# Row norms taken block by block, a third bank for separate products, gate weights split in every chunk, and both z products beside attention, in a two-layer trunk kernel

## The chip, the cores and the metric

The kernel runs on one core of one Trainium2 chip. The metric is the device time of one execution in microseconds. Before the change the median of three runs is 2850.37 us, the lowest 2839.6 and the highest 2852.43.

## The reference

A sequence of 2048 tokens with 1024 channels goes through two layers. Everything is float32. Layer 0 mixes by trailing means, layer 1 by a strictly causal "stick-breaking" attention with 16 heads of 64 channels. Both layers end with a gated embedding.

```python
# layer 0
h = rms_norm(x, a_norm);  u, z = split(h @ a_w_in)
pooled = trailing_means(u, windows 2, 4, 8, 16) - u        # one window per group of 256 channels
x = x + (einsum(pooled, a_w_group) * a_scale * silu(z)) @ a_w_out
x = x + (p[0] @ ple_w[0]) * sigmoid(x @ ple_gate_w[0])
# layer 1
k, v = split(rms_norm(x, kv_norm) @ w_kv);  k = rms_norm_per_head(k, k_norm)
q, z = split(rms_norm(x, b_norm) @ b_w_in); q = rms_norm_per_head(q, b_q_norm)
logits = q k^T / 8          # for s < t only
A[t,s] = sigmoid(logits[t,s]) * prod over s<j<t of (1 - sigmoid(logits[t,j]))
x = x + ((A @ v) * silu(z)) @ b_w_out
x = x + (p[1] @ ple_w[1]) * sigmoid(x @ ple_gate_w[1])
```

## The kernel before, in words

**Tiles.** Activations lie transposed: 128 channels on the partitions, 512 tokens along the free axis. The sequence is cut into four chunks of 512 tokens, numbered 0 to 3. To keep float32 accuracy in matmuls that take a shortened format, every operand is split into a high half (a cast on ScalarE) and a low half (source minus high half, on POOL or VectorE; `split`, lines 187 to 194, and `put_split` for weights, lines 206 to 216). Each product of two tiles is three matmuls: high by high, high by low, low by high. A weight unit of two 128-row tiles is a pair of halves in the pool `wpair`; `pump` (line 250) keeps up to nine units in flight along a list, `plan`. A raw weight goes through a ring of four buffers, `io`, that it shares with residual tiles and others. A unit that is marked `keep` is stored split to memory (`once`) after its first use, and later loads read 512 KB of halves from there; a unit that is not kept is read raw (256 KB) and split again.

**Order of the work.** `opening` does layer 0 for the chunks 0 and 1, then `pair_part(0, 1)`: the v, k and q of both chunks. `attend` then sweeps the heads of the chunks 0 to 2 and threads a stream of other products between the steps of attention: z of chunk 1, and layer 0 of the chunks 2 and 3 except for the gate of chunk 3 (`beside_first`). `middle` does that gate and `pair_part(2, 3)`. The second `attend` does the heads of chunk 3, with z of chunk 3 and the layer ends of the chunks 0 to 2 beside it. The layer end of chunk 3 is last.

**The pair's products.** `job` (line 922) computes v, then k, then q for two chunks at once by a scheme of seven products of half the size instead of eight: p1 to p7, each 48 matmuls of 512 columns. Their operands are mixtures of the activations, which `build` (line 850) makes on VectorE and splits, and mixtures of the weights, which were made once and stored (`mixed`). Some products are added in place in four banks (`total`); p2, p3 and p5 are needed apart and go to the two banks `psl` (`own`). `evacuate` (line 895) reads them out. Ahead of the job `pair_part` computes z of the first chunk of the pair (`gate_z`, line 799), 192 matmuls, while `build` makes its sums.

**The row norms.** `keyed` (line 734) gets four blocks of 128 tokens one after another. For each it squares (ScalarE) and sums by head (VectorE, 8 columns). After the fourth block `rsqrt_mean` (line 177) takes the root of all 32 columns on POOL, as a power of minus one half, and VectorE multiplies the four blocks. The transposes (`finish`) are queued by a list, `lag`, at the earliest 44 steps of TensorE later. They use the two banks `psa`.

**Values.** Attention needs differences of successive rows of v. `valued` (line 709) stores a block of v to memory, loads it back one row later, and POOL subtracts (line 726).

**Order on the engines.** Within one engine instructions run in the order in which they stand. The framework's scheduler sets that order, except that TensorE's instructions in a job and in attention, and the weights' casts, keep the order of the program.

## Time and profile before

| What | Value |
|---|---|
| Profiled execution, its own time | 2840.63 us |
| Its span, first to last instruction | 2838.6 us |
| Mean granted TensorE clock | 0.981 |
| Median of the runs | 2850.37 us |
| Instructions | 38319 |
| Bytes moved | 652.77 MB |

Names in the rows: PE is TensorE, DVE is VectorE, ACT is ScalarE, POOL is GpSimd, SP is SyncE, which issues nearly all transfers. In a group, "out<-in" are the tiles written and read, then come the shapes and the count; behind the first bar are the busy time of all and the mean of one in ns; behind the second is the idle time of the engine ahead of these instructions, and what ended it. In a timeline row the first number is the start and the second the time until the last of the merged instructions ended; matmuls overlap, so the pace is read from start to start. In a row of waits stand the waiting engine, tile and line, what it waited for, the sum, the count and the longest.

`psd`, `psl`, `pso`, `psa` are banks; `total` and `own` are the tiles of the seven products, `pst` is a bank of transposes or of a norm's small sums, `xs` and `xw` are split and raw operands of the job, `rq` is the reciprocal norm of a row, `qs` a block of v, k or q.

### The profile page before, as it was taken

The page shows a single profiled execution, that of the slowest core. Times are in us where ns is not written, and L with a number is a line of the kernel's source. Part 1 is how long each engine was busy: PE and PEld are TensorE (multiplying, and loading weights), DVE is VectorE, ACT ScalarE, POOL GpSimd, SP SyncE. Part 2 cuts the span into 40 slices and gives each one's busy share as a digit, 9 for nine tenths or more (in the row PEclk, how much of TensorE's full clock was granted, in tenths as well). Part 3 has the DMA queues.
Part 4 walks back from the last instruction along what each step waited for, and adds up shares of the span by engine and source line. Part 5 has one row for each costly group of instructions (what it writes and reads, how often), then busy time and mean ns, then how long its engine had stood idle before and what let it go on. Part 6 is the DMA issues. An engine that isn't in the chain of part 4 may idle for free.

```text
span 2838.6 us, 38319 instructions
## 1 busy us (share of the span) xinstructions
PE 2696.2 (95%) x13118; PEld 2215.0 (78%) x13118; DVE 1946.6 (69%) x2479; ACT 1431.3 (50%) x2838; POOL 1038.0 (37%) x737
## 2 busy tenths in 40 slices
PE   9988999889899999999998989999999999999999
PEld 7866888777678887778886777788878878888887
DVE  6733726435458877788545354689999989999952
ACT  5444214345566656545424454566656555666531
POOL 1458513566664425332436655401120111112111
PEclk9999999999999999999999999999999999999999
DMA  7899678575688878767685846865645564566454
GB/s 258 307 401 381 227 243 312 167 248 160 189 308 301 276 246 275 267 214 248 240 284 158 267 148 180 295 188 189 236 157 189 179 208 147 181 192 219 164 186 163
DMA packets 315935, 652.77 MB, mean 230 GB/s; under 512 B 47710, under 2 KB 80478, under 8 KB 315740
## 3 DMA queue, kind: packets, MB, share of 16 engines
q1 hardware_dynamic: 315164, 649.53, 67.6%
q8 instruction: 104, 1.70, 0.2%
q10 hardware_dynamic: 576, 0.79, 0.1%
q14 instruction: 91, 0.75, 0.1%
HBM read 474.56 MB, written 175.64 MB: 229 GB/s over the span
## 4 chain that ended last, share of the span: by engine, by line
PE 37%; DVE 8%; POOL 3%; issue 3%; DMA 3%; ACT 2%; SPq 0%; POOLq 0%; DVEq 0%; ACTq 0%
PE psd L51 18%; PE pso L51 6%; PE psa L55 6%; PE psl L51 6%; DVE pp L1102 4%; DVE at L1122 2%; POOL rq L181 1%; DMA vraw<-qs 1%; POOL xs L189 1%; PE own L51 1%; POOL wpair L210 1%; DVE qs L748 1%; DMA vs<-vraw 0%; ACT at L1120 0%; DVE sg L704 0%
## 5 line engine op out<-in xcount | busy, mean ns | idle before, releaser
L1102 DVE TENSOR_TENSOR_SCAN pp<-pp,floor 128x512 f32<-128x512 f32 (+3 forms) x640 | 752.1, 1211 | 9.5 <-ACT pp L1098 9.5
L1120 ACT CAST at<-psa 128x512 fp32r<-128x512 f32 (+3 forms) x640 | 303.0, 525 | 374.0 <-PE psa L55 371.3
L51 PE MATMUL psd<-x,wpair 128*128 128x512 f32 x1728 | 441.5, 399 | 18.7 <-ACT sg L700 7.7
L1122 DVE TENSOR_TENSOR at<-psa,at 128x512 fp32r<-128x512 f32 (+3 forms) x640 | 358.8, 598 | 138.2 <-ACT at L1120 136.5
L51 PEld LDWEIGHTS psd<-x,wpair 128*128 128x128 f32 x1728 | 328.5, 192 | 96.4 <-ACT sg L700 9.2
L51 PE MATMUL pso<-at,vv 128*128 128x512 f32 (+3 forms) x1280 | 329.2, 371 | 36.6 <-DVE at L1122 32.5
L1098 ACT ACTIVATE pp<-psl 128x512 f32<-128x512 f32 (+3 forms) x640 | 312.9, 550 | 10.3 <-PE psl L51 9.5
L51 PEld LDWEIGHTS pso<-at,vv 128*128 128x128 f32 x1280 | 228.8, 188 | 111.9 <-DVE at L1122 63.7
L51 PE MATMUL psd<-xp,wpair 128*128 128x512 f32 x1248 | 304.3, 392 | 0.4 <-DVE wpair L215 0.2
L55 PE MATMUL psa<-ident,pp 128*128 128x128 f32 x2176 | 294.1, 275 | 0.0
L51 PE MATMUL total<-wpair,xs 128*128 128x512 f32 x1152 | 286.5, 405 | 5.5 <-DVE zr L804 4.2
L55 PEld LDWEIGHTS psa<-ident,pp 128*128 128x128 f32 x2176 | 254.5, 141 | 27.0
L51 PEld LDWEIGHTS psd<-xp,wpair 128*128 128x128 f32 x1248 | 231.8, 188 | 51.0 <-DVE wpair L215 1.4
L1145 POOL TENSOR_TENSOR os<-os,zt 128x512 f32<-128x512 f32 x32 | 54.2, 1694 | 587.6 <-ACT os L1144 540.4
L51 PEld LDWEIGHTS total<-wpair,xs 128*128 128x128 f32 x1152 | 222.1, 196 | 53.5 <-DVE zr L804 5.0
L51 PE MATMUL psl<-kk,qa 128*128 128x512 f32 (+3 forms) x640 | 259.2, 410 | 0.0
L51 PE MATMUL psl<-kk,qb 128*128 128x512 f32 (+3 forms) x640 | 235.2, 368 | 0.0
L51 PE MATMUL own<-wpair,xs 128*128 128x512 f32 x864 | 215.1, 405 | 17.6 <-ACT qs L901 11.2
L51 PEld LDWEIGHTS own<-wpair,xs 128*128 128x128 f32 x864 | 166.7, 196 | 57.4 <-ACT qs L901 15.0
L51 PE MATMUL psd<-og,wpair 128*128 128x512 f32 x744 | 187.7, 392 | 0.0
L51 PE MATMUL psd<-mp,wpair 128*128 128x512 f32 x768 | 181.7, 393 | 3.8 <-ACT wpair L208 3.3
L51 PEld LDWEIGHTS psd<-mp,wpair 128*128 128x128 f32 x768 | 144.7, 189 | 35.3 <-ACT wpair L208 3.7
(145 smaller groups left out, 3998.3 us busy)
## 6 DMA issues: line engine op xcount, KB each, us to landing
wpair<-once SPq DMA_DIRECT2D x348, 512.0 KB, 4.8
kk<-kd SPq DMA_DIRECT2D x160, 256.0 KB, 3.2
vv<-vd SPq DMA_DIRECT2D x160, 256.0 KB, 3.3
once<-wpair SPq DMA_DIRECT2D x68, 512.0 KB, 6.3
wpair<-wf SPq DMA_DIRECT2D x48, 512.0 KB, 5.6
once<-kp SPq DMA_DIRECT2D x36, 512.0 KB, 4.7
vd<-vv SPq DMA_DIRECT2D x32, 512.0 KB, 5.4
kd<-hl SPq DMA_DIRECT2D x64, 256.0 KB, 3.7
```

Source lines behind the costliest of these rows:

```text
L51: return held_in_order(nc.tensor.matmul(*a, **k))
L55: return held_in_order(nc.tensor.transpose(*a, **k))
L181: G.tensor_tensor(out=out_ap, in0=ms, in1=neghalf[:, 0:w], op=ALU.pow)
L189: low = lambda: lo.tensor_tensor(out=half_of(pr, 1), in0=src, in1=f(half_of(pr, 0)), op=ALU.subtract)
L210: (G if state["lo"] % 3 and not state["boot"] else V).tensor_tensor(out=pr[:, 1], in0=raw, in1=f(pr[:, 0]), op=ALU.subtract)
L748: V.tensor_tensor(out=q8, in0=q8, in1=rq[:, 8 * i : 8 * i + 8].unsqueeze(2).to_broadcast([P, 8, HD]), op=ALU.mult)
L1098: A.activation(out=pp[:, r0:], in_=ps[:, :w], func=AF.Sigmoid, scale=-1.0)
L1102: V.tensor_tensor_scan(out=pp[:, r0:][:, ::-1], data0=pp[:, r0:][:, ::-1], data1=least, initial=1.0 if st["diag"] else st["carry"][j], op0 ...
L1120: A.copy(out=at[:, 0, cs], in_=pt[:, cs])
L1122: return lambda: V.tensor_tensor(out=at[:, 1, cs], in0=pt[:, cs], in1=f(at[:, 0, cs]), op=ALU.subtract)
L1145: G.tensor_tensor(out=os, in0=os, in1=zt, op=ALU.mult)
```

## The change

There are five edits.

1. `keyed` takes the root of each block's 8 columns and multiplies that block at once. Four roots of 8 columns stand in place of one of 32.
2. The products apart take turns over three banks: two of `psl` and one of `psa`, from the pair that the transposes use. For v the order of the products is p1, p2, p5, p6, p3, p7, p4.
3. The gate and embedding weights of layer 0 (20 units a chunk) are not kept: no store after the first chunk, and a raw load and a split in every chunk.
4. z of the first chunk of a pair is no longer computed ahead of the job but in the attention after it, ahead of z of the second chunk. `build` takes four of its steps ahead of the job and the others, the splits for p4, in it. It uses the raw tiles that `prefill` left (two loads a step instead of four, into the pool `tmp`). p5's low halves are now split on VectorE. The job's tail reloads all eight tiles of the first chunk, and the attention stream reloads the eight of the second.
5. `prep`, which loads the next chunk's input, puts its norm on the list `lag` when it runs beside attention.

```diff
     def plan_a(s):
-            plan_block("ag", gate_a, b, keep=True)
-            plan_block("al", ple_a, b, keep=True, order=PAIRS[:1])
+            plan_block("ag", gate_a, b)
+            plan_block("al", ple_a, b, order=PAIRS[:1])
...
+    FIRST_PRODUCTS = ("p1", "p2", "p5", "p6", "p3", "p7", "p4")
...
     def keyed(s, kind, b, j, qs):
+        q8 = qs.rearrange("q (h d) -> q h d", d=HD)
         A.activation(out=sq, in_=qs, func=AF.Square)
-        V.tensor_reduce(out=ss[:, 8 * j : 8 * j + 8], in_=sq.rearrange("q (h d) -> q h d", d=HD), op=ALU.add, axis=AX.X)
+        V.tensor_reduce(out=ss, in_=sq.rearrange("q (h d) -> q h d", d=HD), op=ALU.add, axis=AX.X)
+        rsqrt_mean(rq, ss, HD, "q")
+        V.tensor_tensor(out=q8, in0=q8, in1=rq.unsqueeze(2).to_broadcast([P, 8, HD]), op=ALU.mult)
         if j < 3:
             return
-        rsqrt_mean(rq, ss, HD, "q")
-        for i, qs in enumerate(rows):
-            q8 = qs.rearrange("q (h d) -> q h d", d=HD)
-            V.tensor_tensor(out=q8, in0=q8, in1=rq[:, 8 * i : 8 * i + 8].unsqueeze(2).to_broadcast([P, 8, HD]),
-                            op=ALU.mult)
...
     def job(c0, c1):
-                    ps = bank("psl", "own") if apart else totals[j]
+                    if apart:
+                        owns[0] += 1
+                    ps = bank(("psl", "psl", "psa")[owns[0] % 3], "own") if apart else totals[j]
...
     def build(s):
         raws = sets.pop("raw")
         for i in range(4):
-            loads = [scaled(c, kt, row) for c, kt in ((c0, i), (c1, i), (c1, 4 + i), (c0, 4 + i))]
+            (a21, scale1), (a22, scale2) = scaled(s, i, tmp), scaled(s, 4 + i, tmp)
+            a11, a12 = raws[i], raws[4 + i]
...
-            split(sets["p5"][i], a22, G)
+            split(sets["p5"][i], a22, V)
...
     def pair_part(c0, c1):
-        side = build(c0, c1)
-        yield from every(gate_z(c0, sets["p1"] + sets["p2"]), 40, side)
         state["hold"] = True
-        side = reload(c1, 4)
+        side = build(c1)
+        for _ in range(4):
+            next(side)
+        back = reload(c0)
         for n, _ in enumerate(job(c0, c1)):
...
     def beside_first():
-        yield from every(gate_z(1, chunk[1]["x2"]), 18, chunk[2].setdefault("side", prep(2)))
+        yield from z_part(0, reload(1))
+        yield from z_part(1, prep(2))
```

The orders below show three places of the first pair. The first is TensorE, where the job begins. In these rows `psd<-xs` is z of chunk 0, `pst<-ones,acc` and `pst<-ident,r` are the norm of chunk 1, `total` and `own` are p1 and p2. Before:

```order
L51 MATMUL psd<-ple,wpair 128x512 x6
L51 MATMUL psd<-xs,wpair 128x512 x37
L51 MATMUL pst<-ones,acc 128x1 x4
L51 MATMUL psd<-xs,wpair 128x512 x26
L55 MATMUL pst<-ident,r 128x128 x4
L51 MATMUL psd<-xs,wpair 128x512 x129
L51 MATMUL total<-wpair,xs 128x512 x48
```

Now, on the same engine:

```order
L51 MATMUL psd<-ple,wpair 128x512 x6
L51 MATMUL pst<-ones,acc 128x1 x4
L55 MATMUL pst<-ident,r 128x128 x4
L51 MATMUL total<-wpair,xs 128x512 x48
L51 MATMUL own<-wpair,xs 128x512 x96
L51 MATMUL total<-wpair,xs 128x512 x48
```

The 192 matmuls of z have gone, and the norm's matmuls follow the gate's directly; `own` x96 is p2 and p5.

The second place is POOL in the first products of the job. `xs_...` are low halves of the sums, the line with `vs` is the subtraction of shifted values of p2's blocks, and `wpair` is a weight's low half; wpair_4365 is p5's second weight. Before, POOL had this order there:

```order
L189 TENSOR_TENSOR xs_4302<-xw_4632,xs_4302 128x512
L189 TENSOR_TENSOR xs_4301<-xw_4638,xs_4301 128x512
L210 TENSOR_TENSOR wpair_4693<-wraw_4694,wpair_4693 128x512
L210 TENSOR_TENSOR wpair_4771<-wraw_4772,wpair_4771 128x512
L210 TENSOR_TENSOR wpair_4779<-wraw_4780,wpair_4779 128x512
L726 TENSOR_TENSOR vs_4810<-vs_4810,qs_4807 128x512
```

Now POOL has this order:

```order
L189 TENSOR_TENSOR xs_4282<-xw_4277,xs_4282 128x512
L189 TENSOR_TENSOR xs_4307<-xw_3918,xs_4307 128x512
L735 TENSOR_TENSOR vs_4410<-vs_4410,qs_4407 128x512
L189 TENSOR_TENSOR xs_4306<-xw_4131,xs_4306 128x512
L735 TENSOR_TENSOR vs_4428<-vs_4428,qs_4425 128x512
L189 TENSOR_TENSOR xs_4305<-xw_4300,xs_4305 128x512
L210 TENSOR_TENSOR wpair_4365<-wraw_4366,wpair_4365 128x512
```

The weights' low halves stood ahead of the first value subtraction; now p5's second one stands behind two of them.

The third place is VectorE in k, around the first group of norms. L740 and L749 are the sums by head, L748 and L751 the multiplies by `rq`, the L215 and L210 rows are weights. Before:

```order
L740 TENSOR_REDUCE ssq<-sqq 128x8
L215 SCALAR_TENSOR_TENSOR wpair<-wraw,gains,wpair 128x512 x2
L740 TENSOR_REDUCE ssq<-sqq 128x8
L748 TENSOR_TENSOR qs<-qs,rq 128x512 x4
L210 TENSOR_TENSOR wpair<-wraw,wpair 128x512
```

Now, on VectorE:

```order
L749 TENSOR_REDUCE ssq<-sqq 128x8
L911 TENSOR_TENSOR qs<-total,qs 128x512
L215 SCALAR_TENSOR_TENSOR wpair<-wraw,gains,wpair 128x512
L749 TENSOR_REDUCE ssq<-sqq 128x8
L751 TENSOR_TENSOR qs<-qs,rq 128x512
L215 SCALAR_TENSOR_TENSOR wpair<-wraw,gains,wpair 128x512
L210 TENSOR_TENSOR wpair<-wraw,wpair 128x512
L751 TENSOR_TENSOR qs<-qs,rq 128x512 x2
```

The multiplies stood together behind the last sum; now two of four stand behind it, and two weights' low halves stand between.

More of the change, by code (lines that the diff above doesn't have):

```diff
@@ L280, in plan_kinds @@
             b0 = 2 if kind == "v" else 0
-            for name in PRODUCTS:
+            for name in FIRST_PRODUCTS if kind == KINDS[0] else PRODUCTS:
                 for i in range(4):
@@ L533, in prep, with total, spread @@
             yield
-        r = token_norm(ck["acc1"], "x")
-        yield
-        ck["rb1"] = bcast(r, "x")
-        yield
+        if state["solo"]:
+            ck["rb1"] = bcast(token_norm(ck["acc1"], "x"), "x")
+            return
+        def total():
+            ck["r1"] = token_norm(ck["acc1"], "x")
+        def spread():
+            ck["rb1"] = bcast(ck["r1"], "x")
+        lag.append((time["now"] + 12, total))
+        lag.append((time["now"] + 24, spread))
     def gated_late(zr, sg):
@@ L870, in build @@
             split(sets["p3"][i], a12, G)
+            split(sets["p7"][i], a21, G)
+            yield
+        for i in range(4):
+            raw, scale = scaled(s, 4 + i, tmp)
+            yield
+            scale()
+            sets["p4"].append(pair("xs"))
+            split(sets["p4"][i], raw, G)
+            yield
     def mixtures():
@@ L942, in job, with reload @@
                     evacuate(c0, c1, kind, name, j, totals[j], ps, parts)
-    def reload(s, n):
+    def reload(s):
         prs = chunk[s].setdefault("x2", [])
-        for kt in range(n):
+        for kt in range(KT):
             raw, scale = scaled(s, kt, io)
@@ L1027, in beside_first, with z_part @@
         yield from mixed_part(3)
+    def z_part(s, side=()):
+        side = iter(side)
+        yield from every(gate_z(s, chunk[s]["x2"]), 18, side)
+        for _ in side:
+            pass
     def middle():
@@ L1034, in beside_second @@
     def beside_second():
-        yield from gate_z(3, chunk[3]["x2"])
+        yield from z_part(2, reload(3))
+        yield from z_part(3)
         for c in range(NSUB - 1):
```

72 lines of the change are left out of this document (34 added, 38 removed).

## The prediction

> **What bounds the kernel now.** I read the page first, then the busy time of each engine in the stretches of the program, then TensorE's waits in those stretches, then the timelines at the places that the change touches. On the page TensorE is busy for 95% of the span:
>
> ```profile
> PE 2696.2 (95%) x13118; PEld 2215.0 (78%) x13118; DVE 1946.6 (69%) x2479; ACT 1431.3 (50%) x2838; POOL 1038.0 (37%) x737
> ```
>
> That is an average. By stretches (us, then busy us and instructions of PE, PEld, DVE, ACT, POOL, then granted clock, DMA share, GB/s):
>
> ```profile
> 130.00:322.00 192.00, 168.71 (x682) 131.62 (x682) 95.30 (x102) 80.26 (x132) 130.87 (x102) 0.94 0.97 365
> 322.00:455.00 133.00, 133.00 (x587) 109.75 (x586) 54.58 (x77) 26.33 (x48) 40.31 (x37) 1.00 0.70 236
> 455.00:502.00 47.00, 46.55 (x209) 37.84 (x208) 35.90 (x54) 21.99 (x45) 17.14 (x12) 1.00 0.86 317
> 502.00:803.00 301.00, 267.04 (x1137) 211.82 (x1136) 141.72 (x172) 144.17 (x250) 191.13 (x125) 0.95 0.63 196
> 803.00:1409.00 606.00, 585.96 (x2987) 488.05 (x2987) 469.77 (x599) 349.71 (x756) 247.24 (x187) 0.99 0.77 263
> 1504.00:1799.00 295.00, 260.85 (x1110) 207.20 (x1109) 136.79 (x168) 137.22 (x237) 178.95 (x115) 0.94 0.65 203
> 1799.00:2723.00 924.00, 901.83 (x4843) 753.53 (x4841) 841.45 (x1021) 563.70 (x1170) 134.73 (x76) 0.99 0.58 190
> ```
>
> TensorE idles, at a lowered clock, in three places: the end of chunk 0 (first row; DMA share 0.97) and the two seven-product jobs (fourth and sixth rows, 34 us idle each). The z of chunk 0 (455 to 502) and both attentions run close to full. TensorE's waits in the two jobs:
>
> ```profile
> PE pst L55 <- DVE qs L748: 23.5, 22, 5.8
> PE own L51 <- DVE qs L897: 3.4, 1, 3.4
> PE own L51 <- ACT qs L901: 3.2, 5, 1.6
> PE pst L55 <- DVE qs L748: 20.3, 18, 6.1
> PE own L51 <- ACT qs L901: 7.9, 4, 5.3
> ```
>
> Two thirds is one wait: the transposes of normed rows of k and q stand in TensorE's queue and wait for the norm. TensorE's timeline gives the pace and what such a wait costs behind itself:
>
> ```profile
> 455.68 8.71 PE L51 MATMUL psd<-xs,wpair 128*128 128x512 f32 x37
> 501.97 8.56 PE L51 MATMUL total<-wpair,xs 128*128 128x512 f32 x36
> ...
> 569.00 33.10 PE L51 MATMUL total<-wpair,xs 128*128 128x512 f32 x144
> 601.93 5.60 PE L51 MATMUL own<-wpair,xs 128*128 128x512 f32 x24
> ...
> 631.40 2.19 PE L55 MATMUL pst<-ident,qs 128*128 128x128 f32 x4 [5.85 <-DVE qs L748]
> 633.24 2.05 PE L51 MATMUL total<-wpair,xs 128*128 128x512 f32 x4
> 635.09 2.08 PE L51 MATMUL own<-wpair,xs 128*128 128x512 f32 x5
> ...
> 672.99 0.60 PE L55 MATMUL pst<-ident,qs 128*128 128x128 f32 x4
> 673.34 2.33 PE L51 MATMUL total<-wpair,xs 128*128 128x512 f32 x9
> ...
> 796.22 3.37 PE L51 MATMUL psd<-x,wpair 128*128 128x512 f32 x12
> ```
>
> From start to start 144 matmuls take 32.93 us, 0.228 us each; four transposes take 0.35 us at full pace, but 1.84 us behind the 5.85 us wait, and the next four matmuls 1.85 us in place of 0.91. The first job lasts from 501.97 to 796.22, 294.3 us. Its 1008 matmuls need 230 us at full pace and its 28 groups of transposes 10 us, so 54 us are lost, while its waits add up to 33.5 us (23.5, 3.4 and 3.2 above and 3.4 us in single waits): a microsecond of wait costs about 1.6 us. The first kind, v, has its seven products done at 569.00 plus 96 times 0.228, that is 590.9: it takes 88.9 us for 336 matmuls (76.6 us), a loss of 12. The other 42 us are lost in k and q.
>
> **Norms per block and the third bank.** The row norm's root on POOL, at two widths, and the multiply behind it:
>
> ```profile
> L181 POOL TENSOR_TENSOR rq<-ms,neghalf 128x32 f32<-128x32 f32 x16 | 87.2, 5451 | 1.1
> L181 POOL TENSOR_TENSOR r<-ms,neghalf 128x4 f32<-128x4 f32 x8 | 8.2, 1020 | 0.6
> L748 DVE TENSOR_TENSOR qs<-qs,rq 128x512 f32<-128x512 f32 x64 | 63.5, 1051 | 41.9 <-POOL rq L181 41.8
> ```
>
> Between 4 and 32 columns the root costs 0.158 us a column, so at 8 columns I estimate 1.65 us. Behind the last block of a group stand today 5.45 us of root and four multiplies of 1.05 us, 9.7 us; in the changed kernel 1.65 us and, as three blocks are done earlier, one or two multiplies: 3.3 us. The transposes come 44 matmuls (10 us) after that block, and the longest wait is 6.1 us, so 6.4 us less takes nearly all of it away. POOL does four roots for one, 6.6 us for 5.45: 1.2 us for each of 8 groups a job, on an engine that is busy for 191 of 301 us. The Trainium skill ("Perfetto Trace Analysis", Optimizing Scalar/DVE Operations) says that grouping helps where the engine is saturated, and that breaking up lets work finish sooner where the engine makes others wait. By its first half the split would cost 9 us a job; by its second half, on whose side the 23.5 us row stands, it gains.
>
> The most that can go is 21.9 us of transposes' waits a job (mean of 23.5 and 20.3) times 1.6, 35 us. The third bank takes turns with the transposes in one pair of banks, so a transpose can now meet an accumulation that is not yet read: some eight times a job, at the 0.7 us of the add that frees it; and what is late next, the weights' splits, shows already with 0.7 us. I take 28 us a pair for k and q, and 16 to 35 for the range.
>
> **The head of the job.** The z of chunk 0 no longer runs beside the building of the sums. In the changed order nothing stands between the last gate matmul and the norm's small matmuls, and the products follow these. Today's chain from the last output to the turned norm:
>
> ```profile
> 462.00 0.69 DVE L704 TENSOR_TENSOR sg<-sg,xj 128x512 f32<-128x512 f32 x1
> ...
> 471.85 0.60 PE L55 MATMUL pst<-ident,r 128*128 128x128 f32 x4
> ```
>
> These 9.8 us hold some 3 us of queueing behind z. With the sigmoid and product ahead of it TensorE idles for about 8 us at the head; at the jobs' 1.6 it costs 10 to 13, I take 10.5. Then p1 and p2 run (22 us) while the sums are built, and p5 waits for them. What stands in front of p5's second weight, counted from the norm's landing:
>
> ```profile
> L838 DVE TENSOR_TENSOR xw<-xw,rby 128x512 f32<-128x512 f32 x56 | 50.1, 929 | 34.5 <-DMA xw<-x2d 24.1 <-ACT rby L417 9.7 <-POOL wpair L210 0.7
> L189 POOL TENSOR_TENSOR xs<-xw,xs 128x512 fp32r<-128x512 f32 x56 | 89.2, 1612 | 69.5 <-ACT xs L188 69.3 <-PE pso L51 0.2
> ...
> xw<-x2d SPq DMA_DIRECT2D x56, 256.0 KB, 4.2
> ...
> 523.69 0.68 DVE L897 TENSOR_TENSOR qs<-total,qs 128x512 f32<-128x512 f32 x1
> ...
> 534.13 1.30 POOL L726 TENSOR_TENSOR vs<-vs,qs 128x512 f32<-128x512 f32 x1 [5.04 <-DMA vs<-vraw]
> ```
>
> On VectorE 14 steps at 0.93 us to the first difference (13.0); on POOL five splits at 1.61 (8.1) until the buffer of the first raw tile is free for the fourth; its load, 4.2; five VectorE steps to the sum of p2's first block (4.6): 30 us. That block's value goes out to memory and comes back shifted, and POOL subtracts it: 10.4 us from the sum to the subtraction in the two rows above. In POOL's new order two such subtractions and two splits stand ahead of the weight's low half, 7.5 us with it: 48 us. TensorE is there at about 23. With the fastest steps of the rows instead of the means (0.68 and 1.3 us) it is 42. I take a wait of 22 us (10 to 32), 2 us of lowered clock behind it, and 3 us for the last weight of p6, which stands behind the fourth subtraction. The head then takes 10.5 + 76.6 + 22 + 2 + 3 = 114 us, where z and v take 46.3 + 88.9 = 135 now: 21 us less a pair (8 to 36).
>
> **Both z beside attention.** 192 matmuls a pair move there, 43.8 us at 0.228. TensorE's waits there are short, for the second half of the turned weights:
>
> ```profile
> PE pso L51 <- DVE at L1122: 10.9, 16, 2.7
> PE pso L51 <- DVE at L1122: 21.6, 21, 2.7
> ```
>
> More products between them can fill a part; I take 3 us, so 41 (34 to 52). VectorE is busy for 841 of 924 us in the second attention; eight products and eight more scales add 15 us at 0.93, less than TensorE's 41, so TensorE stays the bound. The four further reloads and the deferred norm of the next chunk lie under this too, if there is cover; without it a reload is a split of 1.61 us a tile, 13 us for eight, which the upper end holds.
>
> **Gate weights.** In chunk 0 twenty stores go, of 512 KB each, out of 68:
>
> ```profile
> once<-wpair SPq DMA_DIRECT2D x68, 512.0 KB, 6.3
> ...
> PE psd L51 <- POOL wpair L210: 8.0, 8, 2.1
> PE psd L51 <- ACT sg L700: 7.6, 2, 5.6
> PE psd L51 <- ACT wpair L208: 6.5, 5, 3.3
> ...
> L210 POOL TENSOR_TENSOR wpair<-wraw,wpair 128x512 fp32r<-128x512 f32 x89 | 123.0, 1394 | 90.6 <-ACT wpair L208 88.9 <-DMA mx<-in_w_kv_dram 1.6
> ```
>
> 10.5 MB at the stretch's 365 GB/s are 29 us of transfers; TensorE's 682 matmuls need 155 of these 192 us. So between 0 and 29 us can come back; the splits themselves stay, so I take 12. In the three later chunks each unit's low half costs 1.39 us on POOL, or a step on VectorE, at one unit in 2.7 us of TensorE's work (12 matmuls), with four raw buffers ahead: hidden, at 1 us a chunk for a start that is late (0 to 4, two units waited for in full).
>
> **The sum.** Two pairs at -21, -28 and +41 are -16; chunk 0 is -12 and the splits +3: -25 us. The profiled execution took 2840.6 us, 2 us over its span; its sum is 2815.6. The runs shown lie at 2839.6, 2850.4 and 2852.4, so that time is near their low end; from the middle of the four, 2845.7, the sum gives 2820, which I forecast. For both pairs together the terms reach 28 us (head), 19 (k and q), 18 (attention) and 15 (chunk 0) to a side; added in squares that is 41, and four fifths of it, 33, I take to hold 8 in 10: 2786 to 2852, rounded at the ends.
>
> **Rivals.** *The head's trips queue up (slower).* A load of p6's third and fourth weights waits on SyncE's queue for the very split that is late, and the value stores queue behind it. If the second and third trip through memory do not overlap but follow each other, 10.4 us each, at 1.6, a pair loses 33 us more: 2820 + 66 = 2886. For it: POOL's queue is in order, with the weights behind the subtractions; against it: today's v holds the same four trips and loses 12 us in all. It decides from one and a quarter trips a pair on, where the pairs' gain and chunk 0's are spent.
>
> *The weights are next (no change).* If the wait for the norm only uncovers the splits of the next product's weights, k and q gain 12 us a pair in place of 28: 2820 + 32 = 2852. For it: the 0.7 us wait for a weight beside the longest transposes' wait; against it: in v's last products 144 matmuls run without a gap.
>
> *The loads are light and the cover good (faster).* Chunk 0 gives back the full 29 us, and attention absorbs 10 us more a pair: 2820 - 17 - 20 = 2783. For it: DMA share 0.97 there; against: TensorE at 97% in attention.
>
> The Trainium skill ("TensorE: Matmul & The Clock Gate", Part 1) has the clock halve after an idle window of about 3.4 us. By it only the long waits would carry a surcharge, and by estimate k and q could return at most some 29 us a pair, not 35. The trace has lowered clocks behind shorter waits in a row too (0.95 over the first job).
>
> **Chances.** My forecast 0.58, the queued trips 0.11, the weights 0.18, the light loads 0.13. Half a per cent, 14 us, is about what a measurement of this kernel can tell from no change. Of my own case 0.53 lie below 2836 and 0.05 within; with the fast rival, and 0.03 of the second: faster 0.69, same 0.20, slower 0.11. The range 2786 to 2852 leaves out the slow rival and about half of the fast one.
>
> **What would show it.** In the changed profile: transposes waiting for the norm under 5 us a job; v's p5 beginning with one long wait on POOL's low half of a weight, with the value subtraction ahead of it; the stretch from the last gate matmul to k near 114 us; attention longer by about 41 us each; the end of chunk 0 at a DMA share under 0.9. I am wrong if the head waits less than 10 or over 32 us, if attention grows by under 34, or if k and q still lose over 25 us a job.

## The result and the profile after

The changed kernel takes 2831.7 us (median of 6 runs, 2824.6 to 2834.8), the kernel before 2850.0 (6 runs, 2839.6 to 2852.4): ratio 0.994, 95% interval 0.992 to 0.996. That is 18 us less, where 25 to 30 were forecast. The profiled execution of the changed kernel took 2824.6 us, that of before 2840.6: 16 us, which the rows below account for.

The page after, its first part, then the busy time by stretches (columns as in the prediction; the stretches are chunk 0's end, then head and v of the first pair, its k and q, the first attention with the gate of chunk 3, then the same three of the second pair):

```profile
PE 2671.1 (95%) x13118; PEld 2216.6 (79%) x13118; DVE 2003.3 (71%) x2523; ACT 1477.2 (52%) x2922; POOL 1175.4 (42%) x889
```

```profile
130.00:322.00 192.00, 170.83 (x733) 136.18 (x732) 108.23 (x111) 80.89 (x135) 133.44 (x105) 0.98 0.88 318
...
444.00:546.00 102.00, 86.32 (x353) 69.79 (x352) 60.20 (x67) 40.35 (x72) 72.66 (x49) 0.88 0.64 197
546.00:726.00 180.00, 167.98 (x772) 137.03 (x771) 109.72 (x139) 106.73 (x188) 147.25 (x121) 0.97 0.69 217
726.00:1442.00 716.00, 686.78 (x3425) 574.23 (x3423) 534.43 (x676) 412.72 (x869) 342.73 (x251) 0.98 0.73 253
1442.00:1542.00 100.00, 85.85 (x348) 68.72 (x348) 56.36 (x63) 37.79 (x68) 67.25 (x46) 0.88 0.60 180
1542.00:1750.00 208.00, 175.59 (x776) 142.80 (x775) 112.63 (x139) 110.22 (x191) 167.33 (x134) 0.91 0.67 210
1750.00:2823.00 1073.00, 1049.46 (x5532) 881.86 (x5530) 879.67 (x1070) 585.70 (x1209) 152.71 (x96) 0.99 0.60 197
```

TensorE is busy for 95% as before. Chunk 0's end got lighter (DMA share 0.88 for 0.97, 733 matmuls in the same 192 us for 682). The heads and the k and q of the first pair got shorter, and both attentions longer. But the k and q of the second pair take 208 us at a clock of 0.91, about as long as before, with POOL now busy for 167 us in place of 127. Their stretch in the kernel before:

```profile
1594.00:1799.00 205.00, 180.59 (x774) 142.27 (x773) 99.63 (x125) 101.52 (x175) 126.59 (x78) 0.93 0.66 209
```

This is TensorE's list of waits in that stretch of the changed kernel:

```profile
PE pst L55 <- DVE qs L751: 24.4, 4, 10.7
PE total L51 <- POOL wpair L210: 5.0, 2, 4.0
```

It is the same kind of wait as before, but 24.4 us in four pieces where there were 20.3 in 18. TensorE's timeline at the end of that job shows the two longest:

```profile
1721.21 0.48 PE L55 MATMUL pst<-ident,qs 128*128 128x128 f32 x1 [7.78 <-DVE qs L751]
1721.34 4.19 PE L51 MATMUL total<-wpair,xs 128*128 128x512 f32 x9
1725.33 1.05 PE L55 MATMUL pst<-ident,qs 128*128 128x128 f32 x4
...
1747.57 0.47 PE L55 MATMUL pst<-ident,qs 128*128 128x128 f32 x1 [10.67 <-DVE qs L751]
```

And this is what GpSimd did in front of the last of them. L189 is the low half of a reloaded tile, L765 that of a turned row, L180 and L181 are the root of the last block:

```profile
1738.77 2.48 POOL L189 TENSOR_TENSOR x<-xw,x 128x512 fp32r<-128x512 f32 x2
1741.21 1.26 POOL L765 TENSOR_TENSOR hl<-hl 128x512 fp32r<-128x512 f32 x1
1742.56 0.20 POOL L180 TENSOR_SCALAR ms<-ssq 128x8 f32<-128x8 f32 x1
1742.83 1.95 POOL L181 TENSOR_TENSOR rq<-ms,neghalf 128x8 f32<-128x8 f32 x1
```

VectorE, from that block's sum (L749) to its multiply (L751); L844 scales a reloaded tile:

```profile
1738.72 0.69 DVE L749 TENSOR_REDUCE ssq<-sqq 128x8 f32<-128x512 f32 x1 [2.68 <-POOL ms L180]
...
1744.54 0.69 DVE L844 TENSOR_TENSOR xw<-xw,rby 128x512 f32<-128x512 f32 x1 [1.25 <-DMA xw<-x2d]
...
1746.83 0.68 DVE L751 TENSOR_TENSOR qs<-qs,rq 128x512 f32<-128x512 f32 x1
```

The sum is done at 1739.4, its root begins at 1742.6 behind two reloaded tiles' splits and a turned row's, and is done at 1744.8; the multiply begins at 1746.8, since VectorE first scales tiles that are only just landing. Change 4 put the reload of eight tiles, where there were four, into the last 58 matmuls of the job, on the queues where change 1 had put four roots for one.

The time by stage, in us of the profiled executions, before, after, and of the experiments told below (read from TensorE's timelines; "distance" is how far the transposes stand behind their block; the borders are the last gate matmul of chunk 1, the first z matmul behind the first job, the last gate matmul of chunk 3, the first z matmul behind the second job, and the end):

| kernel | to gate of chunk 1 | head and job 1 | attention 1, chunk 3 | head and job 2 | attention 2, tail | span |
|---|---|---|---|---|---|---|
| before | 455.8 | 340.4 | 662.5 | 340.5 | 1039.4 | 2838.6 |
| after | 444.3 | 281.6 | 715.8 | 307.9 | 1073.2 | 2822.8 |
| norms and bank | 453.7 | 321.9 | 665.6 | 317.5 | 1040.3 | 2799.0 |
| gates kept | 456.3 | 289.0 | 703.3 | 304.8 | 1075.5 | 2828.9 |
| reload's low halves on VectorE | 446.2 | 278.6 | 720.7 | 292.4 | 1073.2 | 2811.1 |
| reload spread | 446.4 | 288.4 | 709.9 | 302.6 | 1074.0 | 2821.3 |
| moves without norms | 447.2 | 311.6 | 713.7 | 324.5 | 1073.3 | 2870.3 |
| norms alone | 455.6 | 320.4 | 664.8 | 316.2 | 1040.2 | 2797.3 |
| bank alone | 457.2 | 344.2 | 662.7 | 340.0 | 1041.1 | 2845.1 |
| distance alone | 457.7 | 323.2 | 676.1 | 325.9 | 1044.1 | 2827.0 |
| norms, bank, distance | 455.1 | 304.8 | 670.6 | 308.6 | 1047.6 | 2786.7 |
| norms, bank, distance, low halves | 455.2 | 309.4 | 667.0 | 306.3 | 1043.2 | 2781.1 |
| the same, more weights on VectorE | 455.6 | 307.8 | 665.7 | 308.3 | 1047.0 | 2784.4 |
| after, distance, low halves | 447.5 | 272.0 | 724.3 | 277.4 | 1082.0 | 2803.2 |

A stage of one and the same code differs by some 2 to 5 us between rows, so single differences of that size say nothing. And each row is one execution: that of the distance alone is the slowest of its six, that of norms, bank and distance the slowest of its five, that of the changed kernel with distance and low halves the fastest of its five.

The gain of 16 us is -11.5 (chunk 0), -58.8 and -32.6 (heads and jobs), +53.3 and +33.8 (attentions).

### The profile page after: what moved, and what is told of

Read it like the earlier page. It is cut to its first block, busy times and chain, and to the rows that moved or that the text cites. A ratio compares the mean times of both kernels' runs of the same rounds, so it can differ in the third digit from the quotient of the medians.

```text
span 2822.8 us, 38660 instructions
## 1 busy us (share of the span) xinstructions
PE 2671.1 (95%) x13118; PEld 2216.6 (79%) x13118; DVE 2003.3 (71%) x2523; ACT 1477.2 (52%) x2922; POOL 1175.4 (42%) x889
## 4 chain that ended last, share of the span: by engine, by line
PE 40%; DVE 9%; POOL 5%; DMA 3%; issue 3%; ACT 2%; SPq 0%; POOLq 0%; ACTq 0%; DVEq 0%
PE psd L51 19%; PE pso L51 7%; PE psl L51 6%; PE psa L55 6%; DVE pp L1126 3%; DVE at L1146 2%; PE own L51 1%; POOL wpair L210 1%; PE total L51 1%; POOL xs L189 1%; DMA wraw<-in_gate_a_dram 1%; POOL rq L181 1%; DVE sg L713 1%; POOL hl L765 1%; DMA xw<-x2d 0%
## 5 line engine op out<-in xcount | busy, mean ns | idle before, releaser
L51 PE MATMUL psd<-x,wpair 128*128 128x512 f32 x2304 | 575.6, 395 | 28.8 <-POOL wpair L210 10.1
L51 PEld LDWEIGHTS psd<-x,wpair 128*128 128x128 f32 x2304 | 432.3, 190 | 126.3 <-POOL wpair L210 13.1
L51 PE MATMUL pso<-at,vv 128*128 128x512 f32 (+3 forms) x1280 | 322.6, 369 | 29.5 <-DVE at L1146 23.9
L210 POOL TENSOR_TENSOR wpair<-wraw,wpair 128x512 fp32r<-128x512 f32 x128 | 180.7, 1420 | 93.6 <-ACT wpair L208 82.8
L702 POOL TENSOR_TENSOR xj<-x 128x512 f32<-128x512 f32 x64 | 105.5, 1653 | 202.5 <-DMA out_dram<-sg 100.9
```

The costliest lines, as they stand in the source:

```text
L51: return held_in_order(nc.tensor.matmul(*a, **k))
L210: (G if state["lo"] % 3 and not state["boot"] else V).tensor_tensor(out=pr[:, 1], in0=raw, in1=f(pr[:, 0]), op=ALU.subtract)
L702: G.tensor_tensor(out=xj, in0=f(x1[o][:, 0]), in1=f(x1[o][:, 1]), op=ALU.add)
```

## The experiments

The theory after the result: norms per block (change 1) do what was forecast, the moved z (change 4, with the deferred norm of change 5, which was not tried by itself) costs more than its heads give, and the reloads at the end of each job take back k's and q's gain. Rivals: the weights' splits are next; four roots for one are late by themselves.

**Norms and bank alone** (the kernel before with changes 1 and 2, `keyed` and the bank's choice as in the changed kernel).

```diff
+        rsqrt_mean(rq, ss, HD, "q")
+        V.tensor_tensor(out=q8, in0=q8, in1=rq.unsqueeze(2).to_broadcast([P, 8, HD]), op=ALU.mult)
...
-                    ps = bank("psl", "own") if apart else totals[j]
+                    if apart:
+                        owns[0] += 1
+                    ps = bank(("psl", "psl", "psa")[owns[0] % 3], "own") if apart else totals[j]
```

> The kernel before with only the norms per block and the third bank; both z, the products' order and the gate weights stay as they were before. Theory: these two edits return the forecast 28 us a pair, and in the changed kernel the second pair's 28 us are lost to the eight reloads (scale on VectorE, split on ScalarE and GpSimd) that now stand among the roots at the end of each job. Then this kernel takes 2850 - 56 = 2794 us (2780 to 2815), less than the changed kernel's 2832, with under 8 us of transposes' waits a job. Rival A, the weights' splits are next: 12 us a pair, 2826 us, with waits for a weight's low half grown to 10 us a job. Rival B, four roots for one on GpSimd's queue make the last group late by themselves: 2840 to 2855 us, with transposes' waits of 6 us and more at the ends of the jobs here too.

2800.8 us (2799.8 to 2812.1), ratio to before 0.985 (0.983 to 0.986): 31 us faster than the changed kernel. So the theory holds in its main part: the changes 3 to 5 together cost more than they bring (change 3 is taken apart below), and the heads and jobs get 18.5 and 23 us shorter than before without them. The waits of its two jobs are not gone, though. Those of the first, then of the second:

```profile
PE pst L55 <- DVE qs L742: 11.8, 4, 5.0
PE total L51 <- POOL wpair L210: 5.5, 2, 3.4
...
PE pst L55 <- DVE qs L742: 6.8, 3, 3.7
PE total L51 <- POOL wpair L210: 6.1, 2, 4.0
```

25.2 us of transposes' waits went (23.5 and 20.3 before), and the two stages got 41.5 us shorter: 1.65 us a microsecond of this wait. Part of both rivals is there too: waits of up to 5 us at the jobs' ends, where four reloads stand among the roots, and some 6 us for a weight.

**Norms alone, bank alone** (the kernel before with change 1, and with change 2).

> The kernel before with the norms per block alone (the third bank left out). With norms and bank together it took 2801 us, 48 less than before. Theory: the transposes' wait was the main loss, so the norms carry some 40 of the 48 us: 2808 us (2800 to 2818), transposes' waits under 12 us a job. Rival A, the two are worth about as much each: 2825 us. Rival B, without the third bank the faster norm only uncovers the wait for a bank that is not yet read (3.4 + 3.2 us and 7.9 us in the jobs of before): 2835 to 2850 us, with those waits doubled.

> The kernel before with the third bank alone (norms grouped as before). Theory: it takes away the waits for an accumulation that is not yet read, 6 to 8 us a job at about 1.6, and may add some 0.7 us waits of transposes for a bank: 2838 us (2828 to 2846), transposes' waits of about 20 us a job as before. Rival A, it is half of what norms and bank gain together: 2825 us. Rival B, products take the transposes' pair of banks, so these wait longer: 2850 to 2860 us.

Norms alone 2806.5 us (2799.2 to 2812.3), ratio 0.986 (0.984 to 0.988); the bank alone 2847.9 us (2841.2 to 2855.2), ratio 1.000 (0.999 to 1.001). The norms carry it. The first job's waits of the bank alone:

```profile
PE pst L55 <- DVE qs L748: 21.9, 23, 4.4
PE total L51 <- POOL wpair L210: 4.1, 2, 2.4
PE total L51 <- DVE qs L897: 3.6, 1, 3.6
...
PE own L51 <- ACT qs L901: 1.5, 1, 1.5
```

The waits of `own` for an unread bank fell from 6.6 to 1.5 us in this job, and others took their place, for a bank of the totals and for a weight. The 10 us expected of the bank are not there. Whether it adds anything to the norms can't be told: the intervals of 2801 and 2806 overlap.

**Gate weights kept** (the changed kernel without change 3).

```diff
-            plan_block("ag", gate_a, b)
-            plan_block("al", ple_a, b, order=PAIRS[:1])
+            plan_block("ag", gate_a, b, keep=True)
+            plan_block("al", ple_a, b, keep=True, order=PAIRS[:1])
```

> The changed kernel with the gate weights of chunk 0 stored again and loaded split in chunks 1 to 3. Theory: the 11.5 us that the stretch up to the last gate matmul of chunk 1 gained (444 in place of 456 us) are the twenty stores of 512 KB: 2843 us (2838 to 2848), that stretch ends near 456 us again. Rival A, the gain comes from the deferred norm of chunk 1 or from the other order of loads: 2832 us, the stretch ends near 444 us. Rival B, splits anew in chunks 2 and 3 cost attention as much as chunk 0 gains: 2832 us as well, but with the stretch ending near 456 us and both attentions shorter by 10 us in sum.

2830.4 us (2824.2 to 2832.4), ratio 0.994 (0.992 to 0.995): no different from the changed kernel. But the place moved as the theory said: the last gate matmul of chunk 1 ends at 456.3, 12 us later, as before. The first attention takes 12 us less, 703.3 us for 715.8; in the changed kernel the gate weights of two chunks are loaded raw and split there. The stretch of the first attention in this kernel:

```profile
745.30:1448.60 703.30, 681.99 (x3425) 571.86 (x3423) 503.73 (x663) 391.14 (x830) 290.97 (x225) 0.99 0.78 272
```

Against the changed kernel's row (534, 413 and 343 us of VectorE, ScalarE and POOL) it has 31, 22 and 52 us less work for the same 3425 matmuls. Rival B is right: change 3 is worth nothing here. On the kernel before, without the moved z, it wasn't tried.

**The reload's low halves on VectorE** (the changed kernel).

```diff
     def reload(s):
-            split(pr, raw, G)
+            split(pr, raw, V)
```

> The changed kernel with the low half of each reloaded tile (z's inputs, eight at the end of each job and eight beside the first z) on VectorE in place of GpSimd. Theory: GpSimd's queue, where the reloads' halves of 1.3 us stand between the roots, makes the transposes late at the jobs' ends (6.6 us in the first, 2.4 + 7.8 + 10.7 us in the second); without them these waits fall under 8 us in sum and the time to 2812 us (2805 to 2820). Rival A: VectorE, which scales the tiles and multiplies the rows, becomes the late one: 2828 to 2840 us, the same waits. Rival B: the reloads' trip from memory is what the queues stand for: 2832 us, unchanged waits.

2812.8 us (2812.6 to 2817.3), ratio 0.988 (0.987 to 0.990), 19 us less than the changed kernel, as the theory said. Its waits in k and q of the second pair:

```profile
PE pst L55 <- DVE qs L751: 9.3, 3, 4.1
```

24.4 us became 9.3 (in the first pair 8.2 became 4.3), and the second pair's stage is 15.5 us shorter; the waits fell less than expected (under 8 in sum), the time as much. In the profiled executions the whole gain is 12 us, since that of the changed kernel was its fastest. This shows that the splits on GpSimd's queue made the transposes late. The Trainium skill ("Perfetto Trace Analysis", Optimizing Scalar/DVE Operations) says that moving work between VectorE and GpSimd might not help, as they share a read port of SBUF. Rows below (the last section) agree on the sharing; the run says that it helped by 19 us here, since what counted was the place in an in-order queue, not the rate.

**The reload spread** (the changed kernel; p3's and p5's buffers handed out first).

```diff
-            if n >= total - 58 and n % 6 == 0:
+            if n >= total - 140 and n % 16 == 0:
                 next(back, None)
```

> The changed kernel with the reloads spread over the last 140 matmuls of a job, one every 16, in place of the last 58, one every 6; the buffers of p3 and p5 are handed out first so that they come free in time. No work changes. Theory: with a reload in 3.7 us in place of 1.4 the roots no longer stand behind two or three splits: transposes' waits at the jobs' ends under 6 us in sum, and z's first matmuls no longer wait for reloaded tiles: 2808 us (2800 to 2820). Rival A: a reload takes one of the four raw buffers from the weights' loads, so that p7 and p4 of q wait for their weights: 2832 to 2845 us, with new waits for a weight. Rival B: the roots themselves, four for one, are the queue: waits of 6 us and more remain, 2825 to 2832 us.

2823.1 us (2817.0 to 2826.7), ratio 0.991 (0.990 to 0.993): 8 us better, not 24; nearest to rival B. Transposes' waits stay at 10.3 and 16.5 us in the two jobs (longest 4.2 and 5.1), so spacing the reloads is not enough; which of the roots, splits and turned rows on the one queue still makes them late was not taken apart. One thing went as expected: z beside the first attention no longer stands for 9.9 us at its start (1.1 us).

**A longer distance** (norms and bank, with the transposes issued 68 matmuls behind the last block; then the low halves of its reloads on VectorE as well).

```diff
-            lag.append((time["now"] + 44, lambda m=m: finish(m)))
+            lag.append((time["now"] + 68, lambda m=m: finish(m)))
```

> The kernel before with norms per block and the third bank, and the transposes of a group issued 68 matmuls after its last block in place of 44 (5.5 us later). Theory: the waits of 11.8 and 6.8 us that norms and bank left at the jobs' ends are a matter of how far the transposes stand behind the roots; with 5.5 us more they fall under 4 us in sum, and at 1.6 the time falls from 2801 to 2778 us (2770 to 2790). Rival A: the transposes are only late somewhere else, in the next kind or the next stage: 2795 to 2805 us. Rival B: the normed rows hold their buffers longer, so that evictions wait and products behind them: 2805 to 2820 us, with waits for qs grown.

> As the last (norms, bank, transposes after 68 matmuls), with the low halves of the reloaded tiles (four at the end of a job here) on VectorE as well. Theory: what is left of the transposes' waits at the ends goes: 2774 us (2765 to 2785), 4 us less than with the longer distance alone. Rival A: the distance alone covers it, so the same time as the last within 4 us. Rival B: VectorE, with the multiply behind each root, is now late: 5 us or more above the last.

2785.4 us (2781.4 to 2788.5), ratio 0.978 (0.976 to 0.980), and 2781.0 us (2778.7 to 2782.9), ratio 0.977 (0.975 to 0.979). The second is the fastest kernel of the study: 67 us faster than the kernel before beside it (2848.0), 51 faster than the changed one. With the distance no transposes' wait is left in either job. The first job's waits with norms, bank and distance:

```profile
PE total L51 <- POOL wpair L210: 5.4, 2, 3.3
```

18.6 us of waits went, the stages of heads and jobs got 26 us shorter, and the attentions 12 us longer. One more group of four transposes stands in each attention (32 for 28), and the waits there grew by 3 us each; that is not the whole 12, and the rest is not explained. About half of the gain stayed in the profiled executions, and the median is 7 us above what was expected. The low halves' 4 us are as expected, but the intervals of the two overlap.

**The distance alone** (the kernel before with only that edit).

> The kernel before with nothing but the transposes after 68 matmuls in place of 44. Theory: the longest wait of before is 6.1 us and the greater distance is 5.5 us, so nearly all of the 23.5 and 20.3 us of transposes' waits go, as they went with norms and bank: 2800 us (2788 to 2812), by distance alone what the norms per block gave. Rival A: behind a grouped root of 5.5 us all four multiplies come in a burst, so the waits only move or the weights are next: 2830 to 2850 us. Rival B: sixteen normed rows hold their buffers longer and evictions wait: 2815 to 2830 us with waits for qs grown.

2821.5 us (2811.9 to 2828.8), ratio 0.990 (0.988 to 0.993). The waits did fall, to 9.4 and 8.4 us, none over 1.3, and in the profiled execution heads and jobs got 31.8 us shorter, but the attentions 18 us longer. That execution was the slowest of the six (2828.8 us, clock 0.977; the others 2811.9 to 2822.4 at 0.980 to 0.985), so part of the 18 is its own. The first job's waits:

```profile
PE pst L55 <- DVE qs L748: 9.4, 10, 1.3
PE own L51 <- ACT qs L901: 4.5, 4, 1.8
PE own L51 <- DVE qs L897: 3.5, 1, 3.5
```

The theory is right in that the waits fell, and wrong on the time. That evictions waited more (rival B) doesn't show: 4.5 and 3.5 us for `own`, 3.2 and 3.4 before. Grouped norms behind a longer distance gave 25 us, norms per block 42 at the old one: the two are not the same thing.

**The moves without the norms** (the changed kernel without changes 1 and 2).

> The changed kernel without its norms per block and without its third bank: z beside attention, the new order of v and the gate weights split anew, with the norms grouped in fours as before. Theory: these edits by themselves cost what they cost beside the fast norms, 31 us (2832 against 2801), and more by the end of the jobs, where the grouped root stands behind the reloads too: 2885 us (2872 to 2900). Rival A: the reloads only hurt the four roots for one, so that without them the moves cost little: 2845 to 2862 us. Rival B: the moves pay by themselves, since the heads gain 34 us a pair: 2820 to 2840 us.

2871.7 us (2868.1 to 2876.2), ratio 1.008 (1.007 to 1.010). The changes 3 to 5 cost 25 us beside the old norms and 31 beside the new ones. The direction is as expected; that they would cost more with the grouped roots is wrong, and so is rival A, that the reloads hurt only the four roots for one.

**The changed kernel with both repairs** (distance and low halves).

> The changed kernel with the two repairs: transposes after 68 matmuls in place of 44, and the reloaded tiles' low halves on VectorE. The same two on the kernel before with norms and bank took 2781 us. Theory: the transposes' waits in the jobs fall under 3 us, so the time falls from the 2813 us of the low halves alone by some 13 us to 2800 us (2792 to 2808), and what is left above 2781 is the price of both z beside attention, 87 us in two attentions for the heads' gain. Rival A: with the repairs the moved z pays: 2770 to 2785 us, level with the other or below. Rival B: the reloads at the end only move into the attention's start, whose waits grow: 2810 to 2820 us.

2810.2 us (2804.9 to 2813.0), ratio 0.987 (0.985 to 0.989). Against low halves alone the stages of heads and jobs are 22 us shorter and the attentions 12 us longer, and the times of all runs can't be told apart. The theory is right on the waits (no transpose waits for a norm in either job) and wrong on the time, which is rival B's; but the attentions' waits grew by only 1 and 5 us, so where the 12 us went is open. Against the same repairs without the moves (2781) it is 29 us slower, though its heads and jobs are 37 and 29 us shorter: its attentions are 57 and 39 us longer.

**More weights' low halves on VectorE** (the fastest kernel, every second instead of every third).

```diff
-            (G if state["lo"] % 3 and not state["boot"] else V)
+            (G if state["lo"] % 2 and not state["boot"] else V)
```

> The fastest so far (the kernel before with norms per block, third bank, transposes after 68 matmuls, reloaded tiles' low halves on VectorE; 2781 us), with every second low half of the split weights on VectorE in place of every third. Theory: the one wait left at k's third product in each job, 5.5 and 6.1 us for a weight's low half on GpSimd, shrinks to 2 us: 2773 us (2766 to 2779). Rival A: VectorE, busy for 800 of 1000 us in attention, makes attention's turned weights late: 2785 to 2800 us. Rival B: the wait is for another step in front of that low half on GpSimd's queue, so nothing moves: 2779 to 2784 us.

2791.0 us (2786.2 to 2794.5), ratio 0.980 (0.978 to 0.982), 10 us slower. The wait for the weight shrank (the first job's rows):

```profile
PE pst L55 <- ACT hl L754: 4.0, 3, 3.1
PE total L51 <- POOL wpair L210: 3.0, 1, 3.0
```

In its place transposes wait for ScalarE to read the bank before. Where the 10 us are is not settled: the profiled executions (2784.4 and 2781.1 us of span), the fastest of the one kernel and the slowest of the other, have stages within 4 us of each other.

## Why the prediction was right, and where it was not

The sum came out near, 16 us in the profile for 25, because its terms missed in opposite directions. That is luck. For both pairs the heads gave -69 us for -42, k and q -22 for -56, and attention with the later splits +87 for +85; chunk 0 gave -11.5 for -12.

The signs that the prediction had set for itself say the same. Of the second pair three of them call it wrong: k and q still lose some 45 us (207.5 less 153 for 672 matmuls at 0.228 and 9 for 25 groups of transposes; over 25 was the sign), the head waits 9.1 us for its weights (under 10), and attention grew by 33.8 (under 34). In the first pair k and q lose 18 us, the head waits 10.3 and attention grew by 53.3: none does. The last two signs of the second pair lie at their limits; the first doesn't.

**The head of the job: right, mis-sized.** Forecast -21 a pair (8 to 36). The first pair's head in the changed kernel, on TensorE:

```profile
442.80 1.52 PE L51 MATMUL psd<-ple,wpair 128*128 128x512 f32 x6
448.03 1.87 PE L51 MATMUL pst<-ones,acc 128*128 128x1 f32 x8 [3.71 <-POOL acc L441]
...
452.30 13.69 PE L51 MATMUL total<-wpair,xs 128*128 128x512 f32 x48
465.82 11.74 PE L51 MATMUL own<-wpair,xs 128*128 128x512 f32 x51
481.85 1.22 PE L51 MATMUL own<-wpair,xs 128*128 128x512 f32 x2 [4.29 <-ACT wpair L208]
489.13 12.69 PE L51 MATMUL own<-wpair,xs 128*128 128x512 f32 x43 [6.05 <-POOL wpair L210]
...
523.70 26.59 PE L51 MATMUL total<-wpair,xs 128*128 128x512 f32 x116
```

The idle head is 8.0 us, as forecast. p5 starts without a wait and then stands for its second weight, 4.3 us for the high half and 6.1 for the low: 10.3 us where 22 were forecast (10 to 32). v ends at 523.70 and 96 times 0.228, 545.6, so head and v take 101.3 us for 135.1 before: -34. The second pair gives -35 (its k then begins with a wait of 2.9 us for a bank, which is counted with k).

The mechanism is the one named in part. The wait for the high half was not in the prediction. ScalarE casts the weights behind the casts of the sums, and these wait for VectorE to make the sums:

```profile
480.14 1.14 ACT L188 CAST xs<-xw 128x512 fp32r<-128x512 f32 x2 [1.05 <-DVE xw L874]
481.19 2.18 ACT L208 CAST wpair<-wraw 128x512 fp32r<-128x512 f32 x4
```

In the second pair it is the larger part, 5.9 us of 9.1:

```profile
1480.47 2.87 PE L51 MATMUL own<-wpair,xs 128*128 128x512 f32 x5 [5.91 <-ACT wpair L208]
```

The wait for the low half is the one that was named. On GpSimd two value subtractions and two splits stand ahead of the weight, and a longer row of splits ahead of these:

```profile
463.64 18.82 POOL L189 TENSOR_TENSOR xs<-xw,xs 128x512 fp32r<-128x512 f32 x10 [8.51 <-ACT xs L188]
482.43 1.75 POOL L735 TENSOR_TENSOR vs<-vs,qs 128x512 f32<-128x512 f32 x1
...
487.81 4.19 POOL L210 TENSOR_TENSOR wpair<-wraw,wpair 128x512 fp32r<-128x512 f32 x3
```

The term that was off is the first leg, 30 us to the sum of p2's first block. VectorE's timeline has that sum here:

```profile
471.56 0.68 DVE L911 TENSOR_TENSOR qs<-total,qs 128x512 f32<-128x512 f32 x1
```

That is 19 us after p1's start. The forecast had put five splits on GpSimd and a load (12.3 us) in series with VectorE's steps; in the trace VectorE runs some 24 steps there, most at 0.6 to 0.8 us, and stands for only 0.4 us. The next leg fits in size, 10.9 us to the subtraction for 10.4, but by luck: it was costed as the value's trip through memory, and here the shifted value was back by 478 (its loads were issued at 474.4 and took 2.5 to 2.9 us), while GpSimd worked without a gap from 463.6 and came to it at 482.4. The queue was what counted, not the trip. The last leg, 6.7 us to the end of the weight's low half, fits (7.5). For p6's last weight (3 us) no wait shows in either pair.

**k and q: this step failed.** Forecast -28 a pair (16 to 35), with transposes' waits under 5 us a job. (The 28 groups of transposes in its loss are 25 in the job before and 7 in the attention behind; its 54 us move by 1.) Measured -25 in the first pair (545.6 to 725.9, for 205.3) and +3 in the second (1542.1 to 1749.6, 207.5 for 204.8), with waits of 8.2 and 24.4 us; the first job's row is

```profile
PE pst L55 <- DVE qs L751: 8.2, 2, 6.6
```

The step that named the weights' splits as what is late next left out the reload of eight tiles that change 4 puts at the end of the job; the prediction priced the "four further reloads" as work under attention (13 us for eight splits, at the upper end), while in k and q GpSimd, busy for 191 of 301 us, was charged 1.2 us a group for its roots and nothing for the splits beside them. The low halves on VectorE showed it (24.4 to 9.3 us), and norms and bank alone gave 18.5 and 23 us. The waits that were left with the low halves on VectorE, and with norms and bank alone, went with the longer distance. Why the second job waits three times as long as the first, with the same eight reloads, is not shown. The 1.6 us for a microsecond of wait came out as 1.65 with norms and bank, but as 1.4 and 1.2 with the longer distance (26 us for 18.6, 31.8 for 26.0) and 1.0 with the low halves on VectorE (18.5 for 19.0): it is no constant.

**Both z beside attention: right, low in the first.** Forecast +41 a pair (34 to 52), measured +53 and +34. Against norms and bank the changed kernel with gates kept adds 38 and 35: this is the moved z with its reloads and the deferred norm. The other 12 us of the first attention come with the gate weights' fresh loads and splits. The longest wait at its start is z's own eviction. TensorE, then ScalarE:

```profile
757.95 2.93 PE L51 MATMUL psd<-x,wpair 128*128 128x512 f32 x6 [9.93 <-DVE zr L810]
```

```profile
753.86 0.62 ACT L188 CAST x<-xw 128x512 fp32r<-128x512 f32 x1 [0.68 <-DVE xw L844]
754.39 0.59 ACT L809 ACTIVATE sg<-psd 128x512 f32<-128x512 f32 x1
```

The sigmoid that frees z's bank stands behind other work of ScalarE, the last of it the cast of a reloaded tile, and this behind its scaling. So the reloads are a part of the 9.9 us; with the reloads spread the wait was 1.1. The prediction asked for cover for the reloads and did not look where they stand in the queue.

**Gate weights: one half right.** Chunk 0 gave -11.5 us for a forecast -12, and its DMA share fell to 0.88 (under 0.9 forecast). The splits in later chunks were put at 1 us a chunk, hidden; keeping the weights showed 12 us in the first attention. That term is 12 for 3, and change 3 is worth nothing.

**The bank.** It was costed inside the term of k and q, without a price of its own. By itself it is worth nothing (0.999 to 1.001).

**The rivals.** The queued trips (2886 us) did not come: p5 waited 10 and 9 us and p6 not at all. The weights as next are there in part: totals' products wait 8.8 us for a weight's low half in the whole changed kernel and 11.6 with norms and bank, 1.3 before. How much of the gain they took was not measured; norms and bank alone still made the two stages 41.5 us shorter of the 56 that were forecast. The light loads came in chunk 0 at 11.5 of 29 us, and attention absorbed 6 to 9 of the 44 us of z (with its reloads).

## What to carry to other kernels

When a step is made shorter and put earlier on an in-order queue, list what else the same change puts on that queue in those microseconds: here one part of a change took back much of what another gave, and one word (which engine splits the reloaded tile) was worth 19 us. Price work that moves "beside" a bound stage at nearly its full length, since 38 and 35 of z's 44 us showed there; it pays only if the place that it leaves was emptier than that. And a total that comes out as forecast doesn't show that its terms did: compare them stage by stage. A leg that comes out as forecast doesn't show its cause either: look at what the step stood behind.

## What was not expected of the hardware

The same VectorE instruction takes 0.68 or some 1.75 us. In the changed kernel's timeline of VectorE, near the end of the second job:

```profile
1707.38 0.68 DVE L751 TENSOR_TENSOR qs<-qs,rq 128x512 f32<-128x512 f32 x1
...
1711.30 1.75 DVE L751 TENSOR_TENSOR qs<-qs,rq 128x512 f32<-128x512 f32 x1
```

and of POOL at the same time:

```profile
1707.60 1.96 POOL L181 TENSOR_TENSOR rq<-ms,neghalf 128x8 f32<-128x8 f32 x1
...
1710.78 1.73 POOL L210 TENSOR_TENSOR wpair<-wraw,wpair 128x512 fp32r<-128x512 f32 x1
```

Beside a root of 8 columns the multiply keeps its 0.68 us; beside a 128x512 split it takes 1.75, and the splits, 1.3 us elsewhere, 1.7. Of the 56 steps of VectorE's scale and multiply (L844, L751) from 1440 to 1750 us, 34 took under 1 us (mean 0.69) and had a 128x512 step of POOL beside them for 14% of their time, 22 took longer (mean 1.60) and had one for 81%. A mean duration hides this: in these rows the price of a VectorE step goes with what GpSimd does beside it.

The root of 8 columns, which no row of before showed, took 1.64 us in most rows of POOL's timeline, for the estimate of 1.65 between 4 and 32 columns. And the pace after a long wait fell by half: behind the 7.8 us wait nine matmuls took 4.0 us, 0.44 us each for 0.228.
